# Two chained transformer blocks on one core: v projections of the latents issued inside the first attention units, and attention outputs, not probabilities, divided by the softmax sums

## The chip, the cores and the metric

The kernel runs on one core of a Trainium2 chip. The metric is the device time of one execution in microseconds (us). The core has a matrix engine (TensorE, PE in the rows), a vector engine (VectorE, DVE), an activation engine (ScalarE, ACT), GpSimd (POOL) and a queue for loads and stores (SyncE, SP), each of which works through its own list of instructions in a fixed order. A wait at the head of such a list holds back all that stands behind it.

## The reference

Two blocks are computed one after the other on 256 rows of 1024 numbers. The first holds MoBA attention, a gated delta rule and a mixture of 4 groups of 8 experts (each row goes to two experts of one group; the kernel works through all 32 experts' weights). The second takes the result as "latents", lets them attend to themselves and to 256 context rows in two ways (A: eight heads with a window, sharing two heads of keys and values, with a sink; B: eight heads with a two-dimensional neighbourhood and a bias), and ends in a SwiGLU feed-forward part. The lines that matter, cut:

```python
h = _modulate(_rms_norm(x, norm1_g[l]), sh1, sc1)            # latents, 256 x 1024
hc = _modulate(_rms_norm(ctx, norm1_g[l]), csh1, csc1)       # context, 256 x 1024
q_a, k_a, v_a, q_b, k_b, v_b = _in_proj(h, w_in[l])
q_ac, k_ac, v_ac, q_bc, k_bc, v_bc = _in_proj(hc, w_in[l])
...
o_a = _window_gqa_latent(q_a, k_a, v_a, k_ac, v_ac, sink_a[l])
o_b = _neighbourhood_latent(q_b, k_b, v_b, k_bc, v_bc, rpb_b[l])
x_new = x + g1 * _merge(o_a, o_b, on_a[l], on_b[l], w_out[l])
h2 = _modulate(_rms_norm(x_new, norm2_g[l]), sh2, sc2)
x_new = x_new + g2 * _swiglu(h2, w_gate[l], w_up[l], w_down[l])

def _window_gqa_latent(q, k, v, k_ctx, v_ctx, sink):
    ...
    p = jax.nn.softmax(jnp.concatenate([s_loc, s_ctx, sink_col], axis=-1), axis=-1)
    ...
    o = (jnp.einsum('bnkgqj,bnjkd->bnqkgd', p_loc, vb)
         + jnp.einsum('bnkgqj,bjkd->bnqkgd', p_ctx, v_ctx))

def _merge(o_a, o_b, g_a, g_b, w_out):
    return jnp.concatenate([_rms_norm(o_a, g_a), _rms_norm(o_b, g_b)], axis=-1) @ w_out
```

Each head has 64 columns. The latents' projection of v for B is the last 512 columns (1792 to 2303) of `w_in`.

## The kernel before

**Weights and the ring.** All weights are loaded by SyncE in blocks of 1 MB (8 KB on each of the 128 partitions). Most go into a ring of nine slots (`NRING = 9`, line 1861), which `load_block` (line 161) takes in turn; a load into a slot is issued when the last reader of what lay there is done. Some of the ring's slots also hold working tiles (`qa`, `qb`, `xf`, `mixed`, the biases, ...). In the last expert steps a few blocks more go to buffers beside the ring, so that 14 places in all hold weights. In the rows `eg`, `eu` and `ed` are gate, up and down weights of experts (four loads of each for one step of four experts), `kv` and `lat` are blocks of 256 columns of the second block's `w_in`, `wq` of its `w_out`, `fg`, `fu`, `fd` of its feed-forward part.

**The expert stage (to about 440 us).** Eight steps, u = 0 to 7. Each computes gate and up (`pgu`) from its `eg` and `eu` and then down (`pyd`) from its `ed`. Between them TensorE computes the context's k and v of the second block, which depend on the inputs alone: `ckbp` from the blocks 1280 and 1536, `cvbp` from 1792 and 2048. So the block 1792 is first loaded in this stage, for the context's v.

**The latents' projections (about 440 to 512 us).** The result `xf` is normalised and transposed; then the projections of the latents run block by block in the order of `LORD = "bav"`: 512 (A's k and v), 1280 and 1536 (B's k), 768 and 1024 (B's q), 0 and 256 (A's q), 1792 and 2048 (B's v, tile `lvbp`). `proj_lat` (line 1547) first has the next block split into a high and a low part (`lath`, `latl`) and then does 48 matmuls of 128x256. Line 1487 loads those of the blocks that were not kept, 1792 among them (a second time), under the name `lat`: five loads.

**The attention (about 512 to 600 us).** Sixteen units: `typ` A then B, four head pairs `m`, two halves `qt` of the queries. For a unit `scores` does the matmuls `sc`, the maximum (DVE), the exponentials with their sums (ACT, into `prs`, `prb` in the rows), the reciprocal of the sums (DVE, line 1645) and multiplies both heads' 128x512 probabilities by it: the first by ACT (line 1650), the second by DVE (line 1652), as `NSC = ("AD",)` says. `turn` transposes them (`ptp`, copied to `pT` by ACT and by DVE), `outputs` multiplies by v into `po` (128x256 for a pair, the outputs transposed). `finish`, once per pair, squares `po` (`osq`), sums it by a matmul with ones (`psq`) and writes `po`, scaled, as a high and a low part (`moh` ACT, `mol` DVE). Of PSUM's eight banks four are the tag `big` (two units' scores), two `tr` (`ptp`), one `sm` (`psq`) and one `mo` (`po`), so `po` of the next pair waits until this pair's is read. The function `hooks(i)` is called behind unit i and issues work for later.

**The output projection (about 575 to 608 us).** `pqa` for A's half and `pqb` for B's half are 128x512 matmuls of `moh` and `mol` with the parts of `wq`; `tmp` and `tmpb` scale them and they are added to x. Then comes the feed-forward part, bound by TensorE to the end.

A scheduler orders the instructions of each engine when the kernel is built, so a change in the text moves instructions elsewhere too. The functions with the change:

Of the kernel before, what the change touches and what calls it, by code (L numbers as in the profile page):

```python
# [12 lines left out]
AF = mybir.ActivationFunctionType  # L13
# [96 lines left out]
def tile_kernel(ctx: ExitStack, tc: tile.TileContext, I, out, dbg=None):  # L110
# [1430 lines left out]
    qa = ring_tile("qa").rearrange("p (i m c) -> p i m c", i=2, m=4)  # L1541

    latw = {512: lka_w, 1280: lkb_w}
    seq = [1280, 1536] + [c for part in LORD for c in {"v": (1792, 2048), "a": (0, 256), "b": (768, 1024)}[part]]
    NEXT = dict(zip(seq, seq[1:]))

    def proj_lat(c0, name):
        hi, lo = latw[c0]
        if c0 in NEXT:
            n = NEXT[c0]  # L1550
            latw[n] = split_w(kvw[n], "lat", pool=PLAT)
        p = pt_([P, 2, 256], "big", name + "p")
        for tt in range(2):
            ts = slice(tt * P, (tt + 1) * P)
            for k in range(8):
                mm3(p[:, tt], hth[:, k, ts], htl[:, k, ts], hi[:, k], lo[:, k], k == 0, k == 7)
        return p
# [3 lines left out]
    def uses(part):  # L1561

        for half in range(2):
            if part == "k":
                yield 1280 + 256 * half, "lkb", lambda p, half=half: qk_heads(p, half, 3, "tr", s=0)
            elif part == "v":
                vs = vb[0][:, :, half * 256:half * 256 + 256]
                yield 1792 + 256 * half, "lvb", lambda p, vs=vs: DVE.tensor_copy(vs, p)
            elif part == "a":
                yield 256 * half, "lq", lambda p, half=half: qk_heads(p, half, 0, "tr", q=qa)  # L1570
            else:
                yield 768 + 256 * half, "lq", lambda p, half=half: qk_heads(p, half, 2, "tr", q=qb)
# [30 lines left out]
    mol = at([P, 8, 256], "htl", "mol", dt=F32R)  # L1603
    rab = []
    ssab = at([P, 2, 2, 4], "ssab", "ssab")

    def scores(typ, m, qt):

# [33 lines left out]
                                       scale=1.0 if typ else 0.125, accum_out=t_[:, 1, s_:s_ + 1])  # L1642
        if typ == 0:
            DVE.tensor_tensor(t_[:, 1], t_[:, 1], t_[:, 3], op=ALU.add)
        DVE.reciprocal(t_[:, 2], t_[:, 1])
        for s_ in range(2):
            r_ = t_[:, 2, s_:s_ + 1]
            e = NSC[(8 * typ + 2 * m + qt) % len(NSC)][s_]
            if e == "A":
                ACT.activation(prs[s_], prs[s_], AF.Copy, scale=r_)  # L1650
            else:
                (POOL if e == "P" else DVE).tensor_scalar(prs[s_], prs[s_], r_, None, op0=ALU.mult)
        return prs,

    def turn(prs):
# [21 lines left out]

    def finish(typ, m, po_):
        k = 4 * typ + m
        osq = at([P, 256], "mt", "osq2", bufs=3)  # L1680
        ACT.activation(osq, po_, AF.Square)
        psq = psm([P, 2], "psq")
        for tt in range(2):
            PE.matmul(psq[:, tt:tt + 1], lhsT=osq[:, tt * P:(tt + 1) * P], rhs=ones1, start=True, stop=True)
        DVE.tensor_copy(ssab[:, typ, :, m], psq)
        ACT.activation(moh[:, k], po_, AF.Copy, scale=onT[:, k:k + 1])
        DVE.scalar_tensor_tensor(mol[:, k], po_, onT[:, k:k + 1], moh[:, k], op0=ALU.mult, op1=ALU.subtract)
        if m == 3:
            ssum = at([P, 2], "ssum", "ssum", bufs=2)
            DVE.tensor_reduce(ssum, ssab[:, typ], axis=AX.X, op=ALU.add)  # L1690
            rab.append(rstd_of(ssum, 2, 1.0 / 512, EPS, f"rab{typ}"))
# [11 lines left out]
    def hooks(i):  # L1703

        nonlocal g1B
        if i in G1U:
            g1B = row_bc(mod[:, 2, :, 0], kvc.tile([P, D], F32, tag="fB", name="g1B"))
        if i in WQU:
# [168 lines left out]
PIN = {"wk0": (2, 3), "wk1": (1, 3), "wo0": (0, 1, 2, 3), "wo1": (0, 1, 2, 3), "wo2": (1, 3), "wo3": (0, 1, 2, 3)}  # L1877
BLK = 0
PLB = (0, 1, 2, 3)
LORD = "bav"  # L1880
AORD = False
LATE = True
G1U = (5,)
# [5 lines left out]
MBN = "wk1"  # L1889
WARM = 16  # L1890
WK1 = True
NSC = ("AD",)
NSM = "DD"
JKA = (True, True)
GB = (3, 4, 5, 6)
# [30 lines left out]
```

## Time and profile before

| what | value |
|---|---|
| time before, median of 3 executions | 812.29 us (810.73 to 813.88) |
| the profiled execution | 814.35 us, of which the span of the profile is 812.6 us |
| busy share of the span: PE, DVE, ACT, POOL | 91%, 53%, 37%, 12% |
| mean granted TensorE clock | 0.972 of 2.4 GHz |
| loads | 201.69 MB, 248 GB/s over the span |

Busy shares are means over stages with different limits. The stages after about 330 us are: experts' weights streaming until 436 us, the latents' projections until 512, attention until 600, output projection until 608, feed-forward until the end. The change touches the text of the second to fourth of these. The rows further down are from the profiled execution.

### The profile page before, as it was taken

What the parts mean: (1) busy time and instruction counts of PE and PEld (TensorE: products, weight loads), DVE (VectorE), ACT (ScalarE), POOL (GpSimd) and SP (SyncE); (2) the same over time, 40 slices, a digit from 0 to 9 for tenths busy, and PEclk for the clock granted to TensorE, in tenths of its full rate; (3) what the DMA queues carried; (4) which work ended last, traced back from release to release, by engine and by line L of the source; (5) the groups of instructions that cost most, each with busy time, mean ns of one, the idle gap of its engine ahead of it and who ended that gap; (6) DMA issues with size and microseconds to landing.
All of it is one profiled execution on the core that took longest, in us unless ns stands there. A gap on an engine that the chain in (4) does not pass through costs nothing.

```text
span 812.6 us, 15311 instructions
## 1 busy us (share of the span) xinstructions
PE 738.1 (91%) x6404; PEld 591.1 (73%) x6404; DVE 431.6 (53%) x972; ACT 300.2 (37%) x532; POOL 94.6 (12%) x84
## 2 busy tenths in 40 slices
PE   7999999999789978589788999899988999999997
PEld 6786887966644435266554899787868999899995
DVE  4776653564712214103223789878666667554554
ACT  5343242453421110101113663598724443344341
POOL 4002000152000000000000476100222000000000
PEclk9999999999799999899889999999998999999999
DMA  7999678577589999999999405111644576856101
GB/s 203 352 375 344 223 260 305 205 298 324 210 335 419 419 418 419 412 403 410 408 408 333 156 20 163 52 52 56 205 156 140 198 255 214 279 185 197 64 2 52
DMA packets 87735, 201.69 MB, mean 248 GB/s; under 512 B 15512, under 2 KB 63056, under 8 KB 75376
## 3 DMA queue, kind: packets, MB, share of 16 engines
q1 hardware_dynamic: 87472, 200.58, 67.0%
q8 instruction: 51, 0.84, 0.4%
q0 software_dynamic: 192, 0.11, 0.1%
q14 instruction: 20, 0.16, 0.1%
HBM read 199.73 MB, written 1.05 MB: 247 GB/s over the span
## 4 chain that ended last, share of the span: by engine, by line
PE 36%; DVE 7%; DMA 7%; ACT 3%; POOL 2%; issue 2%; SPq 1%; DVEq 0%; POOLq 0%; ACTq 0%
PE pfg L103 8%; PE pfu L103 8%; PE pf L103 7%; DMA ed<-in_w_down_dram 3%; DMA kv<-in_w_in_dram 3%; PE ckbp L103 2%; PE ptp L106 2%; PE po L103 2%; PE pqa L103 1%; PE sc L103 1%; PE pqb L103 1%; DMA eg<-in_w_gate_dram 1%; POOL rq L222 1%; PE pgu L103 1%; SPq L168 1%
## 5 line engine op out<-in xcount | busy, mean ns | idle before, releaser
L103 PE MATMUL pfu<-lof,fuh 128*128 128x256 f32 x176 | 50.4, 286 | 0.0
L103 PE MATMUL pfu<-hif,fuh 128*128 128x256 f32 x176 | 50.3, 286 | 0.0
L103 PE MATMUL pfu<-hif,ful 128*128 128x256 f32 x176 | 50.3, 286 | 0.0
L103 PE MATMUL pyd<-ed,hid 128*32 128x512 f32 x256 | 39.5, 628 | 7.5 <-DMA ed<-in_w_down_dram 2.8
L103 PE MATMUL pfg<-hif,fgl 128*128 128x256 f32 x160 | 45.6, 285 | 0.0
L103 PE MATMUL pfg<-hif,fgh 128*128 128x256 f32 x160 | 45.2, 283 | 0.0
L103 PE MATMUL pfg<-lof,fgh 128*128 128x256 f32 x160 | 45.2, 283 | 0.0
L196 DVE TENSOR_TENSOR fdl<-fd,fdh 128x512 fp32r<-128x512 f32 x44 | 27.5, 686 | 29.3 <-ACT fdh L189 29.3
L1389 ACT ACTIVATE sg<-pgu,r1s 128x256 f32<-128x256 f32 x8 | 3.8, 474 | 93.1 <-PE pgu L103 69.2
L189 ACT ACTIVATE fdh<-fd 128x1024 fp32r<-128x1024 f32 x22 | 22.1, 1052 | 41.0 <-issue 41.0
L103 PE MATMUL pgu<-eg,xg 128*32 128x256 f32 x512 | 34.2, 386 | 2.6 <-DMA eg<-in_w_gate_dram 1.5
L103 PE MATMUL pgu<-eu,xg 128*32 128x256 f32 x512 | 33.4, 381 | 2.8 <-DMA eu<-in_w_up_dram 2.8
L103 PE MATMUL pf<-fdl,fh 128*128 128x512 f32 x88 | 35.0, 398 | 0.0
L103 PE MATMUL pf<-fdh,fh 128*128 128x512 f32 x88 | 34.7, 394 | 0.0
L103 PEld LDWEIGHTS pfu<-lof,fuh 128*128 128x128 f32 x176 | 34.3, 195 | 0.0
L103 PEld LDWEIGHTS pfu<-hif,ful 128*128 128x128 f32 x176 | 34.3, 195 | 0.0
L103 PEld LDWEIGHTS pfu<-hif,fuh 128*128 128x128 f32 x176 | 34.2, 194 | 0.0
L103 PE MATMUL pf<-fdh,fl 128*128 128x512 f32 x88 | 34.1, 393 | 0.0
L189 ACT ACTIVATE fuh<-fu 128x1024 fp32r<-128x1024 f32 x22 | 22.1, 1052 | 31.2 <-issue 28.7
L1416 DVE TENSOR_TENSOR yl<-pyd,yh 128x512 fp32r<-128x512 f32 x16 | 11.1, 691 | 40.5 <-ACT yh L1415 33.9
L103 PEld LDWEIGHTS pyd<-ed,hid 128*32 128x32 f32 x256 | 9.6, 112 | 30.5 <-issue 19.8
L103 PEld LDWEIGHTS pfg<-hif,fgh 128*128 128x128 f32 x160 | 30.5, 191 | 0.7 <-issue 0.2
(724 smaller groups left out, 2141.8 us busy)
## 6 DMA issues: line engine op xcount, KB each, us to landing
eg<-in_w_gate_dram SPq DMA_DIRECT2D x32, 1024.0 KB, 16.9
eu<-in_w_up_dram SPq DMA_DIRECT2D x32, 1024.0 KB, 19.8
ed<-in_w_down_dram SPq DMA_DIRECT2D x32, 1024.0 KB, 15.3
wmod<-in_w_mod_dram SPq DMA_DIRECT2D x24, 1024.0 KB, 9.3
fg<-in_w_gate_dram SPq DMA_DIRECT2D x11, 1024.0 KB, 5.4
fu<-in_w_up_dram SPq DMA_DIRECT2D x11, 1024.0 KB, 5.3
fd<-in_w_down_dram SPq DMA_DIRECT2D x11, 1024.0 KB, 4.9
kv<-in_w_in_dram SPq DMA_DIRECT2D x5, 1024.0 KB, 15.7
```

The source lines that it names most:

```text
L103: return self._keep(self.engine.matmul(*args, **kwargs))
L106: return self._keep(self.engine.transpose(*args, **kwargs))
L168: SP.dma_start(v, src)
L189: S_["hi"] = ACT.activation(hf[:, s], vf[:, s], AF.Copy)
L196: i = (POOL if c in pool else DVE).tensor_tensor(lf[:, s], vf[:, s], hf[:, s], op=ALU.subtract)
L222: S_["pow"] = POOL.tensor_tensor(r, v, mhalf[:, :n], op=ALU.pow)
L1389: ACT.activation(sg, pgu[:, 0], AF.Silu, scale=r1s[:, u:u + 1])
L1416: DVE.tensor_tensor(yl, py, yh, op=ALU.subtract)
```

## The change

There are two edits.

1. `"v"` leaves `LORD`. The two projections `lvb` (blocks 1792 and 2048) are issued in `hooks(0)` and `hooks(1)` (`VU = (0, 1)`), into a bank of the tag `sm` instead of `big`; the second result is copied by ACT instead of DVE; the blocks are split at that point. Line 1487 draws its list of loads from `LORD` too, so the second load of 1792 is gone, and the block that was loaded for the context's v keeps its ring slot until the split in `hooks(0)`.
2. The two multiplications by 1/sum per unit are gone. Instead ACT spreads the two reciprocals of a unit to 128x128 (`rr`); in `finish` two transposes by TensorE put a pair's into PSUM (`rows`, 128x256, a tile of the tag `sm` that now also holds `psq`), ACT copies them out, and DVE multiplies `po` by them into `on_`. The square, `moh` and `mol` read `on_`. `on_` takes the tag `qn_` with two buffers, which `tmp0`, `tmp1` and two of the `tmpb` of the output projection also use.

```diff
@@ -1541,15 +1541,17 @@
     qa = ring_tile("qa").rearrange("p (i m c) -> p i m c", i=2, m=4)
 
     latw = {512: lka_w, 1280: lkb_w}
-    seq = [1280, 1536] + [c for part in LORD for c in {"v": (1792, 2048), "a": (0, 256), "b": (768, 1024)}[part]]
+    seq = [1280, 1536] + [c for part in LORD for c in {"a": (0, 256), "b": (768, 1024)}[part]]
     NEXT = dict(zip(seq, seq[1:]))
 
-    def proj_lat(c0, name):
+    def proj_lat(c0, name, p=None):
+        if c0 not in latw:
+            latw[c0] = split_w(kvw[c0], "lat", pool=PLAT)
         hi, lo = latw[c0]
         if c0 in NEXT:
             n = NEXT[c0]
             latw[n] = split_w(kvw[n], "lat", pool=PLAT)
-        p = pt_([P, 2, 256], "big", name + "p")
+        p = p or pt_([P, 2, 256], "big", name + "p")
         for tt in range(2):
             ts = slice(tt * P, (tt + 1) * P)
             for k in range(8):
@@ -1563,9 +1565,6 @@
         for half in range(2):
             if part == "k":
                 yield 1280 + 256 * half, "lkb", lambda p, half=half: qk_heads(p, half, 3, "tr", s=0)
-            elif part == "v":
-                vs = vb[0][:, :, half * 256:half * 256 + 256]
-                yield 1792 + 256 * half, "lvb", lambda p, vs=vs: DVE.tensor_copy(vs, p)
             elif part == "a":
                 yield 256 * half, "lq", lambda p, half=half: qk_heads(p, half, 0, "tr", q=qa)
             else:
@@ -1604,6 +1603,8 @@
     rab = []
     ssab = at([P, 2, 2, 4], "ssab", "ssab")
 
+    sums = {}
+
     def scores(typ, m, qt):
 
         q = (qa, qb)[typ]
@@ -1642,14 +1643,10 @@
                                        scale=1.0 if typ else 0.125, accum_out=t_[:, 1, s_:s_ + 1])
         if typ == 0:
             DVE.tensor_tensor(t_[:, 1], t_[:, 1], t_[:, 3], op=ALU.add)
+        rr = at([P, 2, 64], "rr", "rr", bufs=3)
         DVE.reciprocal(t_[:, 2], t_[:, 1])
-        for s_ in range(2):
-            r_ = t_[:, 2, s_:s_ + 1]
-            e = NSC[(8 * typ + 2 * m + qt) % len(NSC)][s_]
-            if e == "A":
-                ACT.activation(prs[s_], prs[s_], AF.Copy, scale=r_)
-            else:
-                (POOL if e == "P" else DVE).tensor_scalar(prs[s_], prs[s_], r_, None, op0=ALU.mult)
+        ACT.activation(rr, bc(t_[:, 2], 64), AF.Copy)
+        sums[typ, m, qt] = rr.rearrange("p a b -> p (a b)")
         return prs,
 
     def turn(prs):
@@ -1677,9 +1674,17 @@
 
     def finish(typ, m, po_):
         k = 4 * typ + m
+
+        rows_ = psm([P, 258], "rows")
+        for qt in range(2):
+            PE.transpose(rows_[:, qt * P:(qt + 1) * P], sums[typ, m, qt], ident)
+        on_ = at([P, 2, 256], "qn_", "on_", bufs=2)
+        ACT.activation(on_[:, 0], rows_[:, 0:256], AF.Copy)
+        DVE.tensor_tensor(on_[:, 1], po_, on_[:, 0], op=ALU.mult)
+        po_ = on_[:, 1]
         osq = at([P, 256], "mt", "osq2", bufs=3)
         ACT.activation(osq, po_, AF.Square)
-        psq = psm([P, 2], "psq")
+        psq = rows_[:, 256:258]
         for tt in range(2):
             PE.matmul(psq[:, tt:tt + 1], lhsT=osq[:, tt * P:(tt + 1) * P], rhs=ones1, start=True, stop=True)
         DVE.tensor_copy(ssab[:, typ, :, m], psq)
@@ -1703,6 +1708,10 @@
     def hooks(i):
 
         nonlocal g1B
+        if i in VU:
+            half = VU.index(i)
+            vs = vb[0][:, :, half * 256:half * 256 + 256]
+            (ACT.copy if half else DVE.tensor_copy)(vs, proj_lat(1792 + 256 * half, "lvb", psm([P, 2, 256], "lvbp")))
         if i in G1U:
             g1B = row_bc(mod[:, 2, :, 0], kvc.tile([P, D], F32, tag="fB", name="g1B"))
         if i in WQU:
@@ -1877,7 +1886,8 @@
 PIN = {"wk0": (2, 3), "wk1": (1, 3), "wo0": (0, 1, 2, 3), "wo1": (0, 1, 2, 3), "wo2": (1, 3), "wo3": (0, 1, 2, 3)}
 BLK = 0
 PLB = (0, 1, 2, 3)
-LORD = "bav"
+LORD = "ba"
+VU = (0, 1)
 AORD = False
 LATE = True
 G1U = (5,)
@@ -1889,7 +1899,6 @@
 MBN = "wk1"
 WARM = 16
 WK1 = True
-NSC = ("AD",)
 NSM = "DD"
 JKA = (True, True)
 GB = (3, 4, 5, 6)
```

On SyncE the order of the loads in steps 5 to 7 of the expert stage is now another. Before, from the gate weights of step 6 on (`kv_4025` and `kv_4035` are the blocks 1280 and 1536, for the context's k; `kv_4392` is 2048):

```order
L168 DMA eg<-in_w_gate_dram 128x2048 x3
L168 DMA eu<-in_w_up_dram 128x2048
L168 DMA eg<-in_w_gate_dram 128x2048
L168 DMA eu<-in_w_up_dram 128x2048
L168 DMA kv_4025<-in_w_in_dram 128x8x256
L168 DMA eu<-in_w_up_dram 128x2048 x2
L168 DMA kv_4035<-in_w_in_dram 128x8x256
L168 DMA ed<-in_w_down_dram 128x2048 x4
L168 DMA eg<-in_w_gate_dram 128x2048 x4
L168 DMA eu<-in_w_up_dram 128x2048 x4
L168 DMA ed<-in_w_down_dram 128x2048 x4
L168 DMA kv_4392<-in_w_in_dram 128x8x256
```

And the same stretch with the change:

```order
L168 DMA eg<-in_w_gate_dram 128x2048 x3
L168 DMA eu<-in_w_up_dram 128x2048 x2
L168 DMA eg<-in_w_gate_dram 128x2048
L168 DMA eu<-in_w_up_dram 128x2048 x2
L168 DMA kv_4025<-in_w_in_dram 128x8x256
L168 DMA kv_4035<-in_w_in_dram 128x8x256
L168 DMA ed<-in_w_down_dram 128x2048 x4
L168 DMA eg<-in_w_gate_dram 128x2048 x3
L168 DMA eu<-in_w_up_dram 128x2048 x3
L168 DMA eg<-in_w_gate_dram 128x2048
L168 DMA eu<-in_w_up_dram 128x2048
L168 DMA ed<-in_w_down_dram 128x2048 x4
```

The fourth `eg` of step 6 stands one load later and `kv_4025` two loads later. The fourth `eg` of step 7 stands behind three of its `eu`; its slot is now that of an `ed` of step 6, so it, the last `eu` and the first `ed` of step 7 all wait for `pyd` of step 6 (before, only the last `eu` and the `ed` did).

On TensorE at the start of the attention, before: from the last score of unit 3 (`sc_5379`) over those of unit 4 (`sc_5427`, `sc_5428`) with the first transposes of probabilities (`ptp`, of units 0 and 1). All 96 matmuls `lvbp` stand ahead of unit 0's scores.

```order
L103 MATMUL sc_5379<-maskn,identb 128x128
L103 MATMUL sc_5427<-k_3592,qa 128x256 x2
L103 MATMUL sc_5427<-k_4432,qa 128x256 x2
L103 LDWEIGHTS identb
L103 MATMUL sc_5427<-maskc,identb 128x128
L106 MATMUL ptp<-cst,prb_5257 128x128 x4
L106 MATMUL ptp<-cst,prb_5258 128x128 x4
L103 MATMUL sc_5428<-k_3592,qa 128x256 x2
L103 MATMUL sc_5428<-k_4432,qa 128x256 x2
L103 LDWEIGHTS identb
L103 MATMUL sc_5428<-maskc,identb 128x128
L106 MATMUL ptp<-cst,prb_5283 128x128 x4
```

With the change, from the last matmuls `lvbp` over the first transposes to the scores of unit 2 (`sc_5262`, `sc_5263`):

```order
L103 MATMUL lvbp<-lath,hil 128x256
L103 MATMUL lvbp<-latl,hil 128x256
L106 MATMUL pqk<-cst,qr__5086 128x128 x4
L103 MATMUL lvbp<-lath,hil 128x256
L103 MATMUL lvbp<-lath,lol 128x256
L106 MATMUL ptp<-cst,prb_5139 128x128 x4
L103 MATMUL sc_5262<-k_3592,qa 128x256 x2
L103 MATMUL sc_5262<-k_4430,qa 128x256 x2
L103 LDWEIGHTS identb
L103 MATMUL sc_5262<-maskc,identb 128x128
L103 MATMUL sc_5263<-k_3592,qa 128x256 x2
L103 MATMUL sc_5263<-k_4430,qa 128x256 x2
```

Seventy-seven of the 96 `lvbp` matmuls stand ahead of the scores of units 0 and 1 and nineteen behind them; the first transposes stand behind two units' scores, where they stood behind more than four.

On TensorE at the end of the attention, before (the last outputs `po`, the sums of squares, and then the last 12 matmuls of the output projection, of which four are shown):

```order
L103 MATMUL po<-pT_6083,mixed 64x128
L103 MATMUL po<-pT_6076,mixed 64x128
L103 MATMUL po<-pT_6083,mixed 64x128
L103 MATMUL po<-pT_6076,vb_3594 64x128
L103 MATMUL po<-pT_6083,vb_3594 64x128
L103 MATMUL po<-pT_6076,vb_3594 64x128
L103 MATMUL po<-pT_6083,vb_3594 64x128
L103 MATMUL psq<-ones_96,osq_6093 128x1 x2
L103 MATMUL pqb_6171<-wq3h,moh 128x512
L103 MATMUL pqb_6171<-wq3l,moh 128x512
L103 MATMUL pqb_6172<-wq3h,moh 128x512
L103 MATMUL pqb_6172<-wq3l,moh 128x512
```

With the change, the same place:

```order
L103 MATMUL po<-pT_6116,vb_3594 64x128
L103 MATMUL po<-pT_6109,vb_3594 64x128
L103 MATMUL po<-pT_6116,vb_3594 64x128
L106 MATMUL rows<-cst,rr 128x128 x2
L103 MATMUL pqb_6211<-wq2h,moh 128x512
L103 MATMUL pqb_6211<-wq2l,moh 128x512
L103 MATMUL pqb_6211<-wq2h,mol 128x512
L103 MATMUL pqb_6211<-wq2h,moh 128x512
L103 MATMUL pqb_6211<-wq2l,moh 128x512
L103 MATMUL pqb_6211<-wq2h,mol 128x512
L103 MATMUL pqb_6211<-wq3h,moh 128x512
L103 MATMUL pqb_6211<-wq3l,moh 128x512
```

Behind the last `po` there now stand 30 matmuls `pqb` (nine of them ahead of the sums of squares) where there were 12; all twelve of the fourth accumulator come last.

## Rows read from the trace of the kernel before

**Rows 1.** The page, part 2: GB/s moved, in 40 slices of 20.3 us.

```profile
GB/s 203 352 375 344 223 260 305 205 298 324 210 335 419 419 418 419 412 403 410 408 408 333 156 20 163 52 52 56 205 156 140 198 255 214 279 185 197 64 2 52
```

**Rows 2.** SP's issues, 330 to 445 us: start, length, load, count.

```profile
368.00 0.55 SPq L168 DMA_DIRECT2D kv<-in_w_in_dram  x1
370.45 12.48 SPq L168 DMA_DIRECT2D eu<-in_w_up_dram  x2
383.06 0.55 SPq L168 DMA_DIRECT2D kv<-in_w_in_dram  x1
...
399.89 20.81 SPq L168 DMA_DIRECT2D eu<-in_w_up_dram  x4
```

**Rows 3.** Chain that ended last, 340 to 445 us: start, length, what.

```profile
368.00 20.59 DMA kv<-in_w_in_dram
...
424.40 3.60 PE pgu L103 x63
428.00 8.41 DMA ed<-in_w_down_dram
...
```

**Rows 4.** Timeline of PE, 381 to 441 us; idle time before in brackets.

```profile
383.12 3.64 PE L103 MATMUL pgu<-eg,xg 128*32 128x256 f32 x58 [0.68 <-DMA eg<-in_w_gate_dram]
388.72 7.14 PE L103 MATMUL ckbp<-kv,hcT 128*128 128x256 f32 x32 [1.96 <-DMA kv<-in_w_in_dram]
...
403.63 0.39 PE L103 MATMUL pst<-rrT,esel 32*128 32x256 bf16 x1 [3.05 <-DVE kLb L1186]
```

**Rows 5.** Windows: busy us of PE, PEld, DVE, ACT, POOL, PE clock, DMA share, GB/s.

```profile
404.00:406.00 2.00, 2.00 (x6) 1.64 (x6) 1.35 (x4) 0.00 (x0) 0.00 (x0) 0.50 1.00 418
420.00:422.00 2.00, 2.00 (x10) 1.54 (x7) 0.00 (x0) 1.08 (x2) 0.00 (x0) 0.50 0.95 336
```

**Rows 6.** The page, part 6: loads, KB each, median us from issue to landing.

```profile
fg<-in_w_gate_dram SPq DMA_DIRECT2D x11, 1024.0 KB, 5.4
```

**Rows 7.** Timeline of PE at the start of the attention, 512 to 527 us.

```profile
518.11 1.23 PE L103 MATMUL sc<-k,qa 128*128 128x256 f32 x4 [2.25 <-ACT prb L1641]
...
523.31 0.74 PE L103 MATMUL sc<-k,qa 128*128 128x256 f32 x4 [1.12 <-ACT prb L1641]
...
523.96 1.06 PE L106 MATMUL ptp<-cst,prb 128*128 128x128 f32 x8
...
525.89 0.63 PE L106 MATMUL ptp<-cst,prb 128*128 128x128 f32 x4 [0.33 <-DVE st L1645]
```

**Rows 8.** Windows of the start of the attention, columns as in rows 5.

```profile
518.00:521.00 3.00, 2.89 (x13) 2.71 (x14) 2.11 (x6) 2.36 (x9) 0.00 (x0) 0.50 0.03 5
```

**Rows 9.** Instructions by source line: count, shortest, median and longest ns, first and last start.

```profile
L1650 ACT ACTIVATE prb<-prb,st x16: 682/720/808, 523.2 to 581.1; 128x512 f32<-128x512 f32 x16
L1652 DVE TENSOR_SCALAR prb<-prb,st x16: 478/485/882, 523.1 to 580.7; 128x512 f32<-128x512 f32 x16
L1568 DVE COPY mixed<-lvbp x2: 690/690/691, 508.0 to 514.1; 128x512 f32<-128x512 f32 x2
L1687 DVE SCALAR_TENSOR_TENSOR mol<-po,onT,moh x8: 462/478/485, 533.8 to 601.1; 128x256 fp32r<-128x256 f32 x8
```

**Rows 10.** PE, 526 to 601 us: the two rows with a wait over 0.4 us.

```profile
548.39 0.66 PE L106 MATMUL ptp<-cst,prb 128*128 128x128 f32 x4 [0.47 <-ACT g1B L1537]
...
566.61 0.66 PE L106 MATMUL ptp<-cst,prb 128*128 128x128 f32 x4 [1.76 <-ACT pT L1663]
```

**Rows 11.** Timelines of PE, DVE and ACT at the end of the attention.

```profile
600.31 0.39 ACT L1681 ACTIVATE osq<-po 128x256 f32<-128x256 f32 x1 [10.48 <-PE po L103]
601.10 0.48 DVE L1687 SCALAR_TENSOR_TENSOR mol<-po,onT,moh 128x256 fp32r<-128x256 f32 x1 [2.45 <-ACT moh L1686]
602.90 0.39 PE L103 MATMUL pqb<-wq3l,moh 128*128 128x512 f32 x1
603.12 1.07 PE L103 MATMUL pqb<-wq3h,mol 128*128 128x512 f32 x4
606.26 1.83 DVE L1764 TENSOR_TENSOR x<-x,tmpb 128x512 f32<-128x512 f32 x2
```

## The prediction

> **What bounds the kernel now.** I read the page's rates per slice first, then the chain that ended last, then for each stretch that the change reaches the timelines of TensorE and of the load queue. Three things are to be seen. From the 13th slice to the 21st (244 to 427 us) the loads run at 403 to 419 GB/s [rows 1]: there the kernel waits for weights, and the chain goes through loads, a block `kv` that takes 20.59 us from issue to landing and an `ed` that takes 8.41 [rows 3]. TensorE waits for them (1.96 us before `ckbp`) and for a DVE step (3.05 us) [rows 4]. In the attention it is TensorE that is busy: behind 526 us only two waits are over 0.4 us, 0.47 and 1.76 [rows 10]. Only the first ten microseconds of it are broken: waits of 2.25, 1.12 and 0.33 us [rows 7], with the clock at its lower level (0.50, 1.2 GHz) from 518 to 521 [rows 8]. At its end a chain over ACT, DVE and POOL sets when x is done, 606.26 + 1.83 = 608.09 [rows 11]. So the change must be priced in four places: the expert stage (which the diff doesn't name), the start, the middle and the end of the attention.
>
> **The expert stage: a ring slot fewer.** The block 1792 now stays in the ring from its first load until `hooks(0)`; the copy of the projection that reads it starts at 508.0 in the kernel before [rows 9]. Steps 6 and 7 have 13 places where they had 14, and the order of loads shows it: the block 1280 (`kv_4025`) is issued two loads later. At 419 GB/s a block of 1.049 MB takes 2.5 us, so it lands at 368.00 + 20.59 + 5.0 = 393.6 instead of 388.6 [rows 1, 3]. `ckbp` is the next in TensorE's order and starts 4.9 us later than 388.72; behind it stand the rest of step 6's matmuls up to its `pyd`, which in turn frees the slots. In the trace of before, the last `eu` of step 7 is issued when that `pyd` is through: 399.89 + 20.81, less the 0.33 of one issue, is 420.37 [rows 2]. At that moment the queue has just run dry: the window from 420 to 422 is the only one of the stretch with a clear dip, 336 GB/s [rows 5]. With the change that moment is 425.3, while the queue, with the fourth `eg` of step 7 now waiting too, runs dry one block (2.5 us) earlier, at about 418. Six loads remain then, not five. The first comes into an empty queue and takes about 5.2 us (a single 1 MB load of `fg` takes 5.4 [rows 6]), so it lands at 430.5; the 64 matmuls `pgu` on it take 3.60 [rows 3] and end at 434.1. The last two `ed` wait for these, and stand behind an `eu` and two `ed` that land at 433.0, 435.5 and 438.0; they land at 440.5 and 443.0. Before, the last landed at 428.00 + 8.41 = 436.41 [rows 3]. That is +6.6 us. Nothing later takes it back: x after the experts feeds everything up to the attention.
>
> Two bounds. If the second block's late landing were covered after all (the waits of 1.96 and 3.05 us [rows 4] shrinking as others grow), only the missing load would remain: 0 to +2.5. On the other side, TensorE now waits at `ckbp` for up to 6.8 us (386.77, where 383.12 + 3.64 ends, to 393.6) where it waited 1.96, and behind the wait of 3.05 us the clock was at 0.50 during the window from 404 to 406 [rows 4, 5]; four such windows of matmuls at half pace would cost up to another 3 us: +10. I take +6.5, near the walk.
>
> The Trainium skill (TensorE: Matmul & The Clock Gate, "What's actually happening") says that the throttled state is the default and that activity releases it. By that rule a longer wait before `ckbp` is paid twice, as in the upper bound, and this term would be +8 to +10 rather than +6.5; the trace agrees for the wait of 3.05 us (0.50 behind it), and shows no fall behind the one of 1.96.
>
> **The start of the attention.** Before, all 96 `lvbp` matmuls stood ahead of the scores, and TensorE then waited for unit 0's exponentials (2.25 us), since the four banks `big` hold two units' scores. Now 19 of them stand behind the scores of two units and the transposes of unit 0 follow at once, with no normalisation of the probabilities ahead of them. The most to be gained is all waits and the lost half of the slow stretch: 2.25 + 1.12 + 0.33 = 3.70, and 2.89 / 2 = 1.45 for 518 to 521 [rows 7, 8], together 5.2. Against it stands a new wait: both `lvbp` use the one bank `sm`, so the second must wait for the copy of the first (0.69 [rows 9]) behind what DVE has queued; TensorE's first scores also come earlier than 512.67 and meet a `qa` that is no earlier. I take 3.5 off; the bounds are 4.4 and, if the 19 matmuls merely fill the 2.25 us and the copy costs 1, 1.2.
>
> **The middle.** TensorE gets 16 transposes of 128x128. Eight `ptp` in a row take 1.06 us and four 0.63, so one costs 0.43 / 4 = 0.11 [rows 7]: +1.7 us. ACT loses 16 x 0.72 = 11.5 us [rows 9] and gains 16 spreads `rr` and 8 copies of 128x256; from the nearest row (0.39 for a 128x256 `osq` [rows 11]) at most 16 x 0.39 + 8 x 0.39 = 9.4, probably 7. DVE loses 16 x 0.485 + 0.69 = 8.4 and gains 8 multiplications like `mol`, 8 x 0.48 = 3.8 [rows 9]. So ACT and DVE are lighter, by some 4 us each, and the wait of 1.76 us behind ACT's `pT` should go. But TensorE is the busy one here, and relief of the other two pays only by these waits: 0.47 + 1.76 = 2.2. Sum: between -0.5 and +1.7; I take +0.5. The copies of `rows` and the new multiplication are hidden by TensorE's matmuls of the following unit; without that cover a pair would hold `po` longer, and the price is in the second rival.
>
> **The end.** Of the 30 `pqb` behind the last `po` 12 were there before, so 18 move from before the last `po` to behind it. Four take 1.07 and one 0.39, which makes (1.07 - 0.39) / 3 = 0.227 each [rows 11] and 4.1 us for the 18. The last `po` comes earlier by that. Behind it the chain is longer: two transposes, copy (0.39), multiplication (0.48), then square, `moh` and `mol` [rows 11]. `mol` ended 1.3 us behind the last `po`, and will end about 2.7 behind it; the matmuls that need it are 21, not 12, and `tmp0` and `tmp1` have to wait for the tag of `on_`. From the last `po` to x I get 8.9 us where there were 7.8 (600.31 to 608.09 [rows 11]). Net: -4.1 + 1.1 to +1.5, that is -2.6 to -3.0; if the fourth accumulator, whose twelve matmuls now come last, is waited for in full, +1. I take -2.6.
>
> **The sum.** +6.5 - 3.5 + 0.5 - 2.6 = +0.9 us on 814.35, the profiled execution's own time, so 815.3. That execution was 2.06 us above the median of the three runs, 812.29. Put against that median the forecast is 813.2; I say 813. The three runs span 810.7 to 813.9, and 0.5%, 4 us, is about what a measurement can tell from no change. So: no change that can be told, a gain in the attention paid for with a loss where the weights stream.
>
> **The rivals.** The first is that the loss isn't there: the expert stage has enough slack in its queue to absorb the moved loads, at most +1. For it: TensorE is idle some microseconds in this stretch anyway. Against it: the queue was dry already at 420 us and the chain runs through exactly these loads [rows 3, 5]. Then the sum is +1 - 3.5 + 0.5 - 2.6 = -4.6, about 807.5, and with the upper ends of the gains (-4.4, -0.5, -3.0) down to 805. Chance 0.25.
>
> The second is that the normalisation chain becomes a wait: between the last outputs of a pair and the first of the next, `po` (one bank) must now wait for transposes, ACT's copy and DVE's multiplication, which need ACT and DVE just as they are busiest. If each of the eight pairs loses 0.8 us by it (a copy, 0.39, and a multiplication, 0.48, uncovered), the middle costs +1.7 + 6.4 = +8.1 and the sum is +8.5: about 821. It decides from 0.4 us a pair on (+5). For it speaks that 1.76 us were already lost once to a late `pT` [rows 10]; against it that before, `po` was held until `mol` as well, through ACT and DVE alike. Chance 0.17.
>
> The third is the expert stage at its upper bound, +10 with the clock down, and the rest as forecast: +4.4, about 817. Chance 0.18. The forecast itself, within about 4 us of 813, has 0.40.
>
> **The numbers.** Faster by over 0.5% (under 808): most of the first rival and a small share of the forecast, 0.27. Slower (over 816.4): the second rival, most of the third and some of the forecast's upper part, 0.32. Same: 0.41. Cases of both signs hold over half of the chance, so the range is wide: 805 to 820 leaves out the far ends of the first two rivals. The likeliest case's own range is 809 to 817.
>
> **What would show it.** `kv` 1280 landing near 393.6 and the last `ed` near 443, with a hole in the DMA rate between 419 and 426: the first term. The `xf` behind it shifted by the same. TensorE's start of the attention: no wait of 2 us behind the scores and no 0.50 between the first scores and the first `po`; the first outputs `po`, which stand behind the `ptp` of 525.89 now, 3 to 4 us earlier than the expert stage's shift alone would put them. In the middle no wait of over 1 us, `rows` among the releasers of none. At the end x done about 9 us after the last `po`. The forecast is wrong if the last `ed` lands within 2 us of 436.4 (then it is faster), or if `po` or `rows` are waited for in every pair (then it is slower).

## The result and the profile after

The changed kernel takes 823.97 us (median of 4 executions, 823.71 to 824.71) where the kernel before takes 812.48 (median of 4, 810.73 to 813.88): 1.0139 times as long, 95% interval 1.011 to 1.0168. It is slower by 11.5 us, outside the forecast range. The profiled execution has a span of 822.3 us beside 812.6.

The page's rates per slice, after; [rows 1] is the same line of before:

```profile
GB/s 224 343 386 359 225 265 314 124 381 290 185 422 420 419 417 418 407 409 399 419 231 290 150 21 161 52 52 53 204 155 89 236 219 250 257 204 171 87 1 51
```

The 21st slice, 408 before, is 231 now. The windows of the changed kernel show what lies in it (busy us of PE, PEld, DVE, ACT, POOL, PE clock, DMA share, GB/s):

```profile
416.00:418.00 2.00, 2.00 (x20) 0.67 (x18) 0.66 (x1) 0.60 (x1) 0.00 (x0) 1.00 0.27 111
418.00:420.00 2.00, 0.53 (x8) 0.00 (x0) 0.91 (x4) 0.60 (x1) 1.64 (x1) 1.00 0.00 0
420.00:422.00 2.00, 1.17 (x12) 0.49 (x16) 0.68 (x1) 0.00 (x0) 0.00 (x0) 0.88 0.00 0
422.00:424.00 2.00, 2.00 (x13) 0.34 (x6) 0.00 (x0) 0.00 (x0) 0.00 (x0) 0.50 0.00 0
424.00:426.00 2.00, 2.00 (x9) 1.56 (x8) 0.34 (x1) 1.63 (x3) 0.00 (x0) 0.77 0.60 135
```

For 6 us no load is under way at all, and about 8 us are lost with the edges, where before one window dipped to 336 GB/s [rows 5]. SP's issues around it, after:

```profile
371.05 12.73 SPq L168 DMA_DIRECT2D kv<-in_w_in_dram  x2
...
403.64 1.33 SPq L168 DMA_DIRECT2D eu<-in_w_up_dram  x3
423.79 0.33 SPq L168 DMA_DIRECT2D eg<-in_w_gate_dram  x1
```

Between 403.64 + 1.33 and 423.79 SP issues nothing: the fourth `eg` of step 7 is the next in its order and waits for `pyd` of step 6. TensorE in the whole stretch, with idle time and releaser in brackets:

```profile
382.57 5.99 PE L103 MATMUL pgu<-eg,xg 128*32 128x256 f32 x58 [3.16 <-DMA eg<-in_w_gate_dram]
390.79 8.83 PE L103 MATMUL ckbp<-kv,hcT 128*128 128x256 f32 x32 [2.22 <-DMA kv<-in_w_in_dram]
...
442.23 4.33 PE L103 MATMUL pyd<-ed,hid 128*32 128x512 f32 x24 [3.17 <-DMA ed<-in_w_down_dram]
```

and the loads in the chain that ended last:

```profile
371.05 19.60 DMA kv<-in_w_in_dram
...
423.79 4.92 DMA eg<-in_w_gate_dram
...
432.45 9.74 DMA ed<-in_w_down_dram
```

So the block 1280 lands at 371.05 + 19.60 = 390.65 and the last `ed` at 442.19 (436.41 before). Behind that `ed` TensorE has waited 3.17 us, and the first 24 matmuls `pyd` take 4.33 us; before, it waited 1.51 us there and 26 took 3.62:

```profile
436.46 3.62 PE L103 MATMUL pyd<-ed,hid 128*32 128x512 f32 x26 [1.51 <-DMA ed<-in_w_down_dram]
```

The clock is the difference, 1.00 in the window from 436 to 438 before and 0.50 (1.2 GHz) here:

```profile
442.00:444.00 2.00, 1.77 (x12) 0.46 (x16) 0.00 (x0) 0.00 (x0) 0.00 (x0) 0.50 0.77 246
```

The start of the attention on TensorE, after, to be read beside [rows 7]:

```profile
516.71 0.74 PE L106 MATMUL pqk<-cst,qr__5059 128*128 128x128 f32 x4 [3.63 <-DVE qr__5059 L1132]
518.71 0.55 PE L103 MATMUL lvbp<-lath,hil 128*128 128x256 f32 x1 [1.26 <-ACT qa L1180]
...
524.54 0.64 PE L103 MATMUL sc<-k,qa 128*128 128x256 f32 x4
...
533.73 0.66 PE L106 MATMUL ptp<-cst,prb 128*128 128x128 f32 x4 [1.21 <-ACT pT L1660]
```

The waits of 2.25 and 1.12 us are gone; in their place TensorE waits 3.63 us between the two v projections, for DVE's part of q's chain (the steps that make q from its projection), 1.26 us before the second projection, and 1.21 us before the first `po`. The row of 1.26 names ACT's `qa`; DVE's copy of the first projection out of the bank ends at 518.57, 0.14 us before the second starts. The window behind these two waits:

```profile
519.00:522.00 3.00, 3.00 (x15) 3.00 (x15) 2.90 (x8) 0.00 (x0) 0.82 (x2) 0.50 0.88 309
```

so the second projection begins at the lower clock. The end of the attention, after, beside [rows 11]:

```profile
608.01 0.44 PE L106 MATMUL rows<-cst,rr 128*128 128x128 f32 x2
608.20 0.48 PE L103 MATMUL pqb<-wq2h,moh 128*128 128x512 f32 x1
...
615.40 0.39 PE L103 MATMUL pqb<-wq3h,mol 128*128 128x512 f32 x1
617.11 0.94 PE L106 MATMUL pt<-cst,x 128*128 128x128 f32 x6 [1.32 <-POOL x L1771]
```

From the first row on TensorE works without a gap, on the 30 `pqb` and six small matmuls `rows`, until 615.8. On DVE, the last additions to x:

```profile
615.81 1.79 DVE L1773 TENSOR_TENSOR x<-x,tmpb 128x512 f32<-128x512 f32 x1
617.52 0.74 DVE L1769 SCALAR_TENSOR_TENSOR tmpb<-pqb,rab,g1B 128x512 f32<-128x512 f32 x1
618.30 0.69 DVE L1773 TENSOR_TENSOR x<-x,tmpb 128x512 f32<-128x512 f32 x1
```

To split the time by place I take, in every kernel, five starts: the first `lvbp`, the first `po`, the last `po`, the last transpose of x (`pt<-cst,x`), and the last `pf`. Each is the first or last start in the group of that name in the view by line (for the last `pt` that of its weight load). All in us:

| kernel | first `lvbp` at | to first `po` | to last `po` | to last `pt` | to last `pf` |
|---|---|---|---|---|---|
| before | 499.8 | 26.6 | 73.6 | 10.0 | 196.4 |
| after | 507.2 | 27.1 | 73.5 | 12.3 | 196.5 |

The first column holds the expert stage and what follows it. The start of that stage differs from one profiled execution to another by up to 3 us with the same code ahead of it (the first `pgu` at 218.9 before, 216.8 after, 216.0 to 218.8 in the experiments). So the 7.4 us of the column are too few: counted from the first `pgu`, the first `lvbp` comes 280.9 us later before and 290.4 after, 9.5 more. The rest adds 0.5 at the start of the attention, -0.1 in the middle and +2.3 at its end.

### The profile page after: what moved, and what is told of

The parts are those of the page before. It is cut to its first block, busy times and chain, and to the rows that moved or that the text cites. A ratio compares the mean times of both kernels' runs of the same rounds, so it can differ in the third digit from the quotient of the medians.

```text
span 822.3 us, 15349 instructions
## 1 busy us (share of the span) xinstructions
PE 747.1 (91%) x6420; PEld 593.6 (72%) x6420; DVE 428.6 (52%) x963; ACT 297.0 (36%) x541; POOL 94.2 (11%) x84
## 4 chain that ended last, share of the span: by engine, by line
PE 38%; DVE 7%; DMA 7%; ACT 2%; POOL 2%; issue 2%; SPq 1%; DVEq 0%; POOLq 0%; ACTq 0%
PE pfg L103 8%; PE pfu L103 8%; PE pf L103 7%; DMA ed<-in_w_down_dram 3%; DMA kv<-in_w_in_dram 2%; PE ckbp L103 2%; PE pyd L103 2%; PE po L103 2%; PE ptp L106 2%; PE sc L103 2%; PE pqa L103 1%; POOL rq L222 1%; SPq L168 1%; PE pgu L103 1%; PE lvbp L103 1%
## 5 line engine op out<-in xcount | busy, mean ns | idle before, releaser
L103 PE MATMUL pyd<-ed,hid 128*32 128x512 f32 x256 | 42.4, 682 | 8.9 <-DMA ed<-in_w_down_dram 4.3
L196 DVE TENSOR_TENSOR fdl<-fd,fdh 128x512 fp32r<-128x512 f32 x44 | 27.5, 687 | 28.7 <-ACT fdh L189 28.7
L103 PE MATMUL pgu<-eg,xg 128*32 128x256 f32 x512 | 38.1, 418 | 4.7 <-DMA eg<-in_w_gate_dram 3.5
L189 ACT ACTIVATE fdh<-fd 128x1024 fp32r<-128x1024 f32 x22 | 22.1, 1052 | 40.4 <-issue 40.4
L1416 DVE TENSOR_TENSOR yl<-pyd,yh 128x512 fp32r<-128x512 f32 x16 | 11.1, 691 | 45.9 <-ACT yh L1415 38.7
L189 ACT ACTIVATE fuh<-fu 128x1024 fp32r<-128x1024 f32 x22 | 22.1, 1051 | 31.6 <-issue 28.9
L103 PEld LDWEIGHTS pgu<-eg,xg 128*32 128x32 f32 x512 | 18.1, 119 | 20.2 <-issue 5.2
```

The source lines that it names most:

```text
L103: return self._keep(self.engine.matmul(*args, **kwargs))
L189: S_["hi"] = ACT.activation(hf[:, s], vf[:, s], AF.Copy)
L196: i = (POOL if c in pool else DVE).tensor_tensor(lf[:, s], vf[:, s], hf[:, s], op=ALU.subtract)
L1416: DVE.tensor_tensor(yl, py, yh, op=ALU.subtract)
```

## Experiments

The question was which of three things costs the 11.5 us: the ring slot that block 1792 now holds (an effect of the first edit that its text doesn't name), the place of v's matmuls, or the new division. The times are medians; ratios are against the kernel before on the same chip.

**The slot and the two edits apart.** Four kernels make a square. In the first, block 1792 is loaded a second time, as before:

```diff
-    for c0 in [c for part in LORD for c in {"v": (1792,), "a": (0, 256), "b": (768, 1024)}[part]]:
+    for c0 in [c for part in LORD for c in {"v": (1792,), "a": (0, 256), "b": (768, 1024)}[part]] + [1792]:
```

> The changed kernel with one thing undone: block 1792 is loaded a second time among the latents' blocks, so its first copy leaves the ring as in the kernel before (five such loads, and the order of SyncE's loads is that of before). Slot theory: the hole of 8 us in the loads (416.5 to 424.6 us) goes, the first transposes of xf come back from 453.7 to about 446, and the time is 824.0 - 10 = 812 to 816. Rival, that the loss lies in the attention (v matmuls without cover, the new chain in finish) and the later expert stage is chance: 820 to 824.

Measured 815.01 us, ratio 1.0028 (1.0002 to 1.0054): 9.0 us of the loss are gone, and so is the hole (401 to 422 GB/s in its windows from 416 to 424). The second has only the division (`sums`, `rr` and the new `finish`, as in the change), on the kernel before:

> The kernel before with the second edit alone (outputs divided by the sums); v's projections stay where they were. Slot theory: the expert stage is as before; the end of the attention costs about 2 us (18 more matmuls behind the last outputs), 16 transposes up to 1.7 us, less what the lighter ACT and DVE give: 811 to 816. Rival, the chain in finish is the loss: 818 to 824.

Measured 810.2 us, 0.9968 (0.9942 to 0.9993): the second edit alone is a gain of some 2 us (0.6 to 4.7 by the interval), better than I expected. The third has only the first edit (`LORD = "ba"`, `VU` and the hooks):

> The kernel before with the first edit alone: v's projections in the first two units, block 1792 kept in the ring; probabilities are normalised as before. Slot theory: the hole in the loads is there, xf about 7 to 10 us late, and TensorE waits at the start of the attention for q's chain: 819 to 825. Rival, the second edit is the loss: 810 to 815.

Measured 827.37 us, 1.0198 (1.0148 to 1.0249), above what I expected. The fourth is the third with the second load of 1792:

> As the run before, but block 1792 is loaded a second time, so the ring is as before. Slot theory: no hole; what is left is the start of the attention, where the matmuls of the second v projection now stand behind the transposes of q: 811 to 817. Rival as above: 810 to 815 too, so this one tells only beside the run with the kept slot: a difference of 7 to 10 us between the two for the slot theory, none for the rival.

Measured 818.39 us, 1.0075 (1.0051 to 1.0099), above what I expected too. The slot costs 824.0 - 815.0 = 9.0 us with the division and 827.4 - 818.4 = 9.0 without it. Moving v, at an unchanged ring, costs 818.4 - 812.5 = 5.9 without the division and 815.0 - 810.2 = 4.8 with it; the intervals can't tell these two apart.

**The slot alone.** If the slot is the cause, taking the second load away must cost the same with no matmul moved and no division changed. The edit is one entry in a line of the kernel before:

```diff
-    for c0 in [c for part in LORD for c in {"v": (1792,), "a": (0, 256), "b": (768, 1024)}[part]]:
+    for c0 in [c for part in LORD for c in {"v": (), "a": (0, 256), "b": (768, 1024)}[part]]:
```

> The kernel before with neither edit, only without the second load of block 1792: the first copy stays in the ring until its split for the latents, all matmuls stay where they were. The order of SyncE's loads is that of the changed kernel. Slot theory: a hole of about 8 us in the loads and 9 us on the time, 820 to 822, though a load of 1 MB less is done. Rival (the slot costs only together with v's later split in the attention): 811 to 814.

Measured 821.14 us, 1.0105 (1.0087 to 1.0124): 9.0 us for one load of 1 MB less. Its windows have the same hole (columns as above):

```profile
418.00:420.00 2.00, 2.00 (x12) 1.26 (x14) 0.00 (x0) 0.33 (x1) 0.00 (x0) 1.00 0.32 131
420.00:422.00 2.00, 1.49 (x16) 0.26 (x8) 0.86 (x2) 0.71 (x2) 0.72 (x1) 1.00 0.00 0
422.00:424.00 2.00, 0.22 (x4) 0.19 (x8) 1.38 (x2) 0.16 (x1) 0.91 (x1) 1.00 0.00 0
424.00:426.00 2.00, 2.00 (x16) 0.31 (x8) 0.00 (x0) 0.00 (x0) 0.00 (x0) 0.75 0.00 0
426.00:428.00 2.00, 2.00 (x11) 1.61 (x8) 0.00 (x0) 1.25 (x2) 0.00 (x0) 0.50 0.49 86
```

The slot's cost lies ahead of the first `lvbp`. Counted from the first `pgu`, that comes 11.1 us later than in the kernel before; in the other two pairs (1792 kept against loaded again) the difference is 9.7 us with both edits and 9.4 with the first alone. From the first `lvbp` on this kernel has the code of before, and reads 25.6, 73.6, 10.0 and 195.0 us between the starts of the first table, where the kernel before reads 26.6, 73.6, 10.0 and 196.4. So a single trace can be off by 1 us or more in one of these columns.

**The start of the attention.** With the ring restored, what does moving v cost? My theory was that TensorE lost its cover: before, 73 of the 96 `lvbp` matmuls stood ahead of q's first transposes, now 48, since the second projection needs the bank `sm` (copied out by DVE) and its split. First the split is made ahead of time again:

```diff
     seq = [1280, 1536] + [c for part in LORD for c in {"a": (0, 256), "b": (768, 1024)}[part]]
+    seq += [1792, 2048]
     NEXT = dict(zip(seq, seq[1:]))
```

> The run with both edits and 1792 loaded again, and the blocks 1792 and 2048 split into high and low parts ahead of time, as in the kernel before. Cover theory (the second v projection's matmuls no longer stand ahead of the transposes of q, because they wait for the one bank sm to be copied out and for their split, so TensorE waits for q's chain uncovered): only one of its two causes is taken away, the transposes still stand ahead: 812 to 815, a part of the 5 us. Rival (v's work in the first units loads DVE and ACT, the order doesn't matter): 815 as with the late split.

Measured 811.09 us, 0.9995 (0.9974 to 1.0017), better than expected. Then ACT also copies the first projection out:

```diff
-            (ACT.copy if half else DVE.tensor_copy)(vs, proj_lat(
+            (DVE.tensor_copy if half else ACT.copy)(vs, proj_lat(
```

> As the run before, and the first v projection is copied out by ACT, which is idle there, the second by DVE. Cover theory: the second projection can start within 1 us of the first, but four transposes of q still stand ahead of it on TensorE: 811 to 814. Rival: 815.

Measured 809.54 us, 0.9968 (0.9947 to 0.9989), again better than expected. And then q's first transposes are ordered behind the 24th matmul of the second projection (an earlier part of the edit, behind the dots, collects these transposes in `S_`):

```diff
...
-                mm3(p[:, tt], hth[:, k, ts], htl[:, k, ts], hi[:, k], lo[:, k], k == 0, k == 7)
+                m_ = mm3(p[:, tt], hth[:, k, ts], htl[:, k, ts], hi[:, k], lo[:, k], k == 0, k == 7)
+                if c0 == 2048 and (tt, k) == (0, 7):
+                    for t_ in S_["pqk00"][-4:]:
+                        after(t_, m_)
```

> As the run before, and the transposes of q's first half are ordered behind the 24th matmul of the second v projection, so that TensorE's order is nearly that of the kernel before (72 matmuls, transposes, 24 matmuls, transposes, scores). Cover theory: the loss at the start is gone and the time is that of the second edit alone, 809 to 812. Rival: 814 to 816.

Measured 810.3 us, 0.9981 (0.9959 to 1.0003): no better than the run before it. So my theory falls in one half. The order on TensorE is not what costs: with q's transposes ahead, TensorE waits 2.27 us there; with them behind, it waits 2.39 us further on, for unit 0's exponentials (the two kernels' timelines of PE):

```profile
505.68 0.63 PE L106 MATMUL pqk<-cst,qr__5069 128*128 128x128 f32 x4 [2.27 <-DVE rqv L220]
```

```profile
517.36 0.66 PE L106 MATMUL ptp<-cst,prb 128*128 128x128 f32 x4 [2.39 <-ACT prb L1647]
```

What costs is that the split comes late. In the run with the reload and the late split TensorE waits 3.63 us for q's transposes, as in the changed kernel, and 1.38 us for the copy of the first projection:

```profile
511.10 0.55 PE L103 MATMUL lvbp<-lath,hil 128*128 128x256 f32 x1 [1.38 <-DVE mixed L1714]
```

With the split made early it waits 2.25 and 0.18 us:

```profile
505.12 0.63 PE L106 MATMUL pqk<-cst,qr__5069 128*128 128x128 f32 x4 [2.25 <-DVE rqv L220]
505.92 0.36 PE L103 MATMUL lvbp<-lath,hil 128*128 128x256 f32 x1 [0.18 <-DVE mixed L1715]
```

And behind the longer waits the clock is down:

```profile
512.00:514.00 2.00, 2.00 (x11) 2.00 (x10) 1.94 (x7) 0.00 (x0) 0.20 (x1) 0.50 0.90 369
```

With the split early it is 1.00 behind the waits (window from 506 to 509). The first 28 matmuls of the second projection start within 5.90 us (511.10 to 517.00) at the lower clock and within 3.31 us (505.92 to 509.23) at the higher. From the first `lvbp` to the first `po` the two runs take 27.5 and 22.1 us; of these 5.4 us, 2.6 are the waits and 2.6 the clock. By the medians alone (1.0028 and 0.9995) the step is hardly clear of the intervals; the next, to 0.9968, is.

Why is q's chain late? With the late split, DVE and POOL at that place read:

```profile
500.27 0.69 DVE L1120 TENSOR_TENSOR qn__5051<-lqp,rq 128x512 f32<-128x512 f32 x1 [1.53 <-POOL rq L222]
502.52 2.96 DVE L1129 TENSOR_TENSOR rt<-qn__5051,mixed 128x128 f32<-128x128 f32 x4
```

```profile
502.31 2.61 POOL L196 TENSOR_TENSOR latl<-kv,lath 128x512 fp32r<-128x512 f32 x2 [0.81 <-ACT lath L189]
```

Four small multiplications of q's rotation (`rt`) take 2.96 us while POOL makes two low parts beside them. Ahead of them, q's normalisation waits 1.53 us for a POOL result, `rq`, which stood behind another low part in POOL's list (0.20 us in the kernel before). To see whether POOL is the reason, the late split was given to DVE alone:

```diff
-            latw[c0] = split_w(kvw[c0], "lat", pool=PLAT)
+            latw[c0] = split_w(kvw[c0], "lat", pool=())
```

> Both edits with block 1792 loaded again and the late split, but the low parts of the two v blocks are made by DVE alone, none by POOL. In the late split two POOL instructions of 1.3 us run beside the four small DVE multiplications of q's rotation (rt), which take 2.96 us there and 1.0 us elsewhere. Theory that POOL slows them: rt takes 1.0 us, though DVE has four more parts of 0.7 us to make; the time is 811 to 815. Rival, that they are slow for another reason, such as the place: rt still takes 3 us, 815 to 818.

Measured 812.35 us, 1.0003 (0.9987 to 1.0018). The same four multiplications there:

```profile
498.22 0.90 DVE L1129 TENSOR_TENSOR rt<-qn__5051,mixed 128x128 f32<-128x128 f32 x4
```

They take 0.90 us for 2.96, DVE no longer waits for `rq`, and TensorE waits 0.64 us for q's transposes where it waited 3.63. From the first `lvbp` to the first `po` it is 23.2 us for 27.5, although DVE has more to do and the copy of the first projection now costs TensorE a wait of 2.59 us. So the traces show POOL as the reason. The medians (1.0028 and 1.0003) can't price it: the step is within their intervals.

**The end of the attention.** The second edit alone costs 3 us between the last `po` and the transposes of x. If the longer chain of `finish` is the reason, the old way for the last pair alone should give them back:

```diff
+        if (typ, m) == (1, 3):
+            for s_ in range(2):
...
+                    ACT.activation(prs[s_], prs[s_], AF.Copy, scale=r_)
...
+                    DVE.tensor_scalar(prs[s_], prs[s_], r_, None, op0=ALU.mult)
...
```

> The second edit alone, but the last of the eight pairs is normalised in the old way (probabilities multiplied by 1/sum, outputs read from PSUM). Tail theory (the longer chain from the last outputs to mol pushes 18 matmuls of the output projection behind the last outputs, and this costs 3 us there): 12 matmuls stand behind the last outputs again and the time is 2 to 3 us below the second edit's alone, 807 to 809. Rival (TensorE does the same work in either order, so nothing is lost there): 810 to 811.

Measured 811.65 us, 0.9987 (0.9965 to 1.0009), no gain. The end is short again, and the middle is longer by as much:

| kernel | first `lvbp` at | to first `po` | to last `po` | to last `pt` |
|---|---|---|---|---|
| division alone | 499.3 | 22.1 | 72.7 | 13.1 |
| the same, last pair the old way | 499.4 | 22.0 | 76.8 | 9.5 |
| both edits, 1792 loaded again | 499.5 | 27.5 | 73.6 | 12.0 |
| v moved alone, 1792 loaded again | 498.0 | 31.3 | 74.8 | 10.0 |
| neither edit, 1792 kept | 510.1 | 25.6 | 73.6 | 10.0 |
| both, loaded again, split early | 496.9 | 22.1 | 74.2 | 13.6 |
| the same, first copy by ACT | 497.5 | 20.0 | 74.6 | 13.2 |

From the first `po` to the last transpose of x it is 85.8 us with the division alone, 86.3 with the last pair the old way, and 83.6 before: TensorE does the same matmuls on one side of the last `po` or on the other.

## Why the prediction was wrong

**The expert stage** (+6.5 forecast, 9.0 measured): right in kind, too small. The ring slot, the late block 1280, the queue that runs dry (forecast about 418, seen at 416.5) and the late last `ed` came. The cost is shown by three pairs of kernels. That the last `ed` landed at 442.2, close to the forecast 443.0, is in part luck: the walk was held against the trace of before as if both began alike, while the changed execution had its first `pgu` 2.1 us earlier. Counted from there the last `ed` is 7.9 us late, not 6.6, and the block 1280, which landed at 390.65 and not at 393.6, is 4.2 late, not 5.0.

The mis-sized term is the lower clock, which I set aside as the upper bound. It was paid. `ckbp` took 8.83 us where it took 7.14 [rows 4]. And behind the wait for the last `ed`, 3.17 us for 1.51, the clock fell: from that landing to the transposes of `xf` it took 11.5 us where it took 10.0. With 7.9 + 1.5 the transposes of `xf` come 9.4 us later, counted from the first `pgu`. The matmuls `pgu` on the late `eg` were slow as well, 5.99 us for 58 where they took 3.64, but that is hidden: TensorE still waited 2.22 us for the block 1280 behind them. The other figure that the prediction gave for this term, +8 to +10, is where it came out.

**The start of the attention** (-3.5 forecast, +0.5 measured): this is the step that failed. I put the gain down to the 19 matmuls that stand behind the scores together with the missing normalisation, with a copy of 0.69 us as the price; that TensorE would meet a `qa` that is no earlier I named and gave no price. The square takes the two apart. The gain of 4.5 us (26.6 to 22.1) comes with the division alone: the transposes of unit 0 no longer wait for the normalisation. About 1.1 us of it are no gain but moved work: before, the scores of five units stood ahead of the first `po` (40 matmuls `sc<-k,qa`), with the division alone those of four (32), and a unit's scores take 1.13 us in the changed kernel (525.66 to 526.79). TensorE still waits 2.26 us there, but only once:

```profile
517.56 0.66 PE L106 MATMUL ptp<-cst,prb 128*128 128x128 f32 x4 [2.26 <-ACT prb L1643]
```

and the clock stays at 1.00 behind it. Moving v costs 4.7 us (26.6 to 31.3) without the division and 5.4 (22.1 to 27.5) with it. I had named the bank and its copy but not that the split of the two blocks moves as well, from ahead of the projections into the middle of q's chain on DVE and POOL. A moved step was priced without the instructions of other engines that it issues, and without the clock behind the new waits, which is half of the cost.

**The middle and the end** (+0.5 and -2.6 forecast, together -2.1; -0.1 and +2.3 measured, together +2.2): the failed step is "The last `po` comes earlier by that". The 18 matmuls did move behind the last `po`, but the last `po` came at most 0.9 us earlier (73.6 to 72.7 with the division alone), so the 4.1 us credited for them were not there. Other work took their place: with the division alone the two stretches together are 2.2 us longer, of which the 16 transposes are 1.7 at the forecast's price of 0.11 each and the unit's scores that now stand behind the first `po` 1.1, less 0.6 of waits (1.76 + 0.47 before, 1.1 + 0.5 now). I had counted the chain behind the last `po` as if it, and not TensorE, set the end. `mol` did end 2.7 us behind the last `po`, as forecast, but the 30 `pqb` end 7.7 us behind it, at 615.8. Then the last `tmpb` stands on DVE behind an addition of 1.79 us, so that x is done 10.9 us behind the last `po` (608.08 to 618.99) and not 8.9: the full wait for the fourth accumulator, +1, which I had named and not taken.

**The sum.** The three misses are 2.5, 4.0 and 4.3 us, 10.8 in all, and the forecast of +0.9 on top gives the 11.5 measured to within 0.2. That it closes so well is luck: the first comes from medians, the others from single traces, which can be off by 1 us in one column. The second rival (waits for `po` or `rows` in every pair) didn't occur; none of TensorE's waits in the attention of the changed kernel names them. The third (expert stage at its upper bound) nearly did, and alone would have given 817.

Two versions beat the kernel before: the change with 1792 loaded again, split early and copied by ACT, 0.9968 (0.9947 to 0.9989), and the second edit alone, 0.9968 (0.9942 to 0.9993). So moving v gains nothing that can be told from the second edit.

## What to carry to other kernels

A list of loads that is drawn from the same table as the order of the work is part of the change: ask what each tile that is now loaded once, and not twice, holds on to meanwhile. Saving a transfer can cost several, where the saved buffer was the one that let the next loads go. When a step is moved, move its preparation in your reckoning too, on every engine, and price a new wait of TensorE with the clock behind it, at the rate of a row that shows it. And matmuls that change sides of a mark save nothing while TensorE is busy on both.

## What the runs showed of the hardware

DVE and POOL can stand in each other's way. The 128x128 multiplications `rt` take 0.28 us each alone, and up to 1.38 us when POOL subtractions of about 1.3 us run beside them (count, shortest, median and longest ns, of the run with the reload):

```profile
L1129 DVE TENSOR_TENSOR rt<-qn__5051,mixed x4: 280/764/1380, 502.5 to 505.2; 128x128 f32<-128x128 f32 x4
L1129 DVE TENSOR_TENSOR rt<-qn__5078,mixed x4: 286/287/293, 513.1 to 513.8; 128x128 f32<-128x128 f32 x4
```

The Trainium skill (SBUF — State Buffer, "Who interferes with whom") says that VectorE and GpSimd share one pair of ports under an exclusive lock, and that a VectorE instruction with two inputs in SBUF contends with a GpSimd instruction that reads SBUF. The trace agrees: the longest multiplication is most of a POOL instruction longer than the shortest (1.38 - 0.28 = 1.10 us of 1.3), and without POOL the four take 0.90 us together. The addition to x at 615.81, beside one of POOL's, takes 1.79 us for 0.69, again 1.10 more. In the kernel before, the same two subtractions ran beside the two `qb` (502.31 to 503.82), which read one of their inputs from PSUM: those took 1.51 us together, as they do elsewhere without POOL, and `rt` behind them took 1.00. So by these traces it is the place in time that costs: in the late split the subtractions fell beside `rt`.
